# A 2-D prefix-sum diagonal kernel: the end of the last batch rearranged over blocks 30 to 32, and block 32 of the other batches loaded in one piece

## The chip, the cores and the metric

The kernel runs on one core of one Trainium2 chip. The metric is the device time of one execution in microseconds (us). A core has TensorE (PE in the profile, with its weight loads as PEld), VectorE (DVE), ScalarE (ACT), GpSimd (POOL), SyncE (SP), which here issues the loads, and 16 DMA engines. Time before: 684.33 us, median of 3 runs (683.99 to 684.5). Ratios compare runs of the same chip and rounds; where two experiments of different rounds are set side by side, the kernel before, at 684.2 to 684.4 us in all rounds, is the link.

## The reference

```python
def setup_inputs():
    B, H, W = 4, 4224, 4224
    return {"x": np.random.randn(B, H, W).astype(np.float32)}

def reference(x):
    ps = np.cumsum(np.cumsum(x, axis=1), axis=2)
    diag = np.diagonal(ps, axis1=1, axis2=2)
    return np.cumsum(diag, axis=1).astype(np.float32)
```

The output is only 4 x 4224 numbers, but all of x has to be read: 285 MB. The step from one diagonal element of the 2-D prefix sum to the next is a row sum up to the diagonal plus a column sum above the diagonal. So the kernel needs one number s per row, and then two running sums over all 4224 rows: one gives the diagonal, the next gives the output.

## The kernel before

Each batch is cut into 33 blocks of 128 rows (P = 128, W = 4224, LAST = 32). A block arrives as one tile of 128 x 4224. ScalarE sums its rows up to the diagonal block. VectorE multiplies the diagonal block with a strict upper triangle (`du`) and adds the columns to the right to a running `acc`. TensorE gets the column sums from `du` and `acc` with a vector of ones.

```python
        for I in range(NB):
            is_last = I == LAST
            xt = tiles.tile([P, W], FP32, name="xt")              # 6 buffers
            if not is_last or len(last_chunks) == 1:
                nc.sync.dma_start(out=xt, in_=x[b, P * I : P * (I + 1), :])
            else:                                                 # block 32: four pieces
                for (c0, c1) in last_chunks:                      # 256, 1792, 1920, 256 columns
                    nc.sync.dma_start(out=xt[:, c0:c1], in_=x[b, P * I : P * (I + 1), c0:c1])
            # ... ScalarE: row sums (block 32: four sums into rp_parts)
            nc.vector.tensor_tensor_reduce(out=du, in0=xt[:, P * I : P * (I + 1)], in1=u_strict,
                                           # ...
                                           accum_out=rp_du[:, I : I + 1])
            nc.tensor.matmul(cp_ps[:, I : I + 1], lhsT=du, rhs=ones_col, ...)
            if I >= 1:
                nc.tensor.matmul(cp_ps[:, I : I + 1], lhsT=acc[:, P * I : P * (I + 1)], rhs=ones_col, ...)
            # ... VectorE: acc[:, P*(I+1):] += xt[:, P*(I+1):]
```

At the end of every batch the two running sums ("pass 1" and "pass 2") are made for blocks 0 to 31 as soon as block 31 has been summed. Each pass is a chain of small matmuls with small copies between them, on ScalarE: `a_sb`, `p_sb`, then `a2_sb`, `p2_sb`. Block 32 enters at the very end, with one matmul against a ramp: the two running sums are linear in s, so row sums that come late can be added afterwards.

```python
    def cumsum_pass1(x_sb):
        nc.tensor.matmul(cs_ps, lhsT=u_incl, rhs=x_sb, start=True, stop=False)
        nc.tensor.matmul(a_ps, lhsT=x_sb, rhs=ones_col, start=True, stop=True)
        nc.scalar.copy(a_sb, a_ps)
        nc.tensor.matmul(p_ps, lhsT=a_sb, rhs=u_strict[0:NB, 0:NB], start=True, stop=True)
        nc.scalar.copy(p_sb, p_ps)
        nc.tensor.matmul(cs_ps, lhsT=ones_row, rhs=p_sb, start=False, stop=True)
        nc.vector.tensor_copy(t_sb, cs_ps)
    # ...
        nc.tensor.matmul(ot_ps[LAST : LAST + 1, :], lhsT=delta, rhs=ramp_ut, ...)   # block 32
        nc.scalar.copy(ot_sb[LAST : LAST + 1, :], ot_ps[LAST : LAST + 1, :])
        nc.scalar.dma_start(out=out_by_block[b, LAST : LAST + 1, :], in_=ot_sb[LAST : LAST + 1, :])
```

## Time and profile before

| | before |
|---|---|
| span of the profiled run | 682.8 us |
| last piece of input landed (from the DMA's semaphore in the trace) | 674.20 us |
| from there to the end | 8.6 us |
| busy: DVE, ACT, PE | 48%, 42%, 22% |

The page of the profile cuts the span into 40 slices. The DMA row gives the busy share of the 16 DMA engines in tenths, the row below what they moved in GB/s; the two lines after these are the chain of work that ended last, by engine and by what it did.

```profile
DMA  8999999999999999999999999999999999999992
GB/s 364 432 430 430 428 429 427 426 431 424 429 428 428 426 430 426 430 429 429 423 429 428 428 429 430 430 429 431 427 420 429 430 426 430 431 428 429 428 424 112
...
DMA 88%; DVE 6%; ACT 4%; issue 1%; PE 0%; SPq 0%; DVEq 0%; ACTq 0%
```

The stream of input bounds the kernel from start to end. No engine is near full. What is outside the stream is the tail. The timeline of the tail gives start, duration, engine, line, operation, result and operands with their shapes, and in brackets the idle time before it and what ended it:

```profile
669.16 3.62 ACT L138 ACTIVATE act_scratch<-xt 128x4096 bf16<-128x4096 f32 x1 [1.52 <-DMA xt<-in_x_dram]
...
672.77 0.40 ACT L146 ACTIVATE act_scratch<-xt 128x256 bf16<-128x256 f32 x1
672.90 0.19 DVE L216 TENSOR_TENSOR s_sb<-rp_full,rp_du 128x32 f32<-128x32 f32 x1 [2.98 <-ACT act_scratch L138]
...
673.17 1.68 ACT L146 ACTIVATE act_scratch<-xt 128x1792 bf16<-128x1792 f32 x1
...
675.56 1.80 ACT L146 ACTIVATE act_scratch<-xt 128x1920 bf16<-128x1920 f32 x1
...
677.75 0.13 ACT L106 COPY a_sb<-a_ps 33x1 f32<-33x1 f32 x1
...
679.14 0.26 ACT L235 COPY ot_sb<-ot_ps 32x128 f32<-32x128 f32 x1 [0.72 <-PE ot_ps L113]
...
679.45 0.59 PE L272 MATMUL ot_ps<-ramp_ut,delta 128*1 128x128 f32 x2 [0.34 <-ACT ot_sb L235]
...
680.07 0.26 ACT L280 COPY ot_sb<-ot_ps 1x128 f32<-1x128 f32 x1 [0.68 <-PE ot_ps L272]
680.36 0.21 ACTq L281 DMA_DIRECT2D out_dram<-ot_sb  x1
```

ScalarE does nearly everything in turn: block 31's sum, the four sums of block 32, and the small copies of both passes between them (`a_sb` of pass 2 has to wait until 677.75, behind the sums). The last input landed at 674.20, but the last copy ends only at 680.33, and the span 2.5 us after that.

### The profile page before, as it was taken

The numbers are of one execution on the slowest core, as the hardware profiler recorded it, in microseconds if no ns is written. First come the engines' busy times: TensorE is split into PE (matmuls) and PEld (weight loads), VectorE is DVE, ScalarE is ACT, GpSimd is POOL, SyncE is SP. The second block draws the span as 40 slices with busy tenths as digits, with TensorE's granted clock in tenths as the row PEclk, the third lists the DMA queues.
The fourth block names the chain that finished last, engine by engine and source line by source line (L and its number), as shares of the span: only waits on it lengthen the run. The fifth ranks groups of instructions, "written<-read, shape, count | busy, mean of one in ns | idle before, by whom it ended". The sixth has DMA issues, their size and how long they took to land.

```text
span 682.8 us, 2551 instructions
## 1 busy us (share of the span) xinstructions
PE 146.8 (22%) x592; PEld 129.1 (19%) x592; DVE 327.0 (48%) x432; ACT 285.8 (42%) x313; POOL 9.2 (1%) x17
## 2 busy tenths in 40 slices
PE   0121121122311211211322112112132112122123
PEld 0121121122211211211212112112121112111122
DVE  3876553321587664422167765433117766543211
ACT  1122344567312333556712223446671123345566
POOL 1000000000100000000010000000001000000000
DMA  8999999999999999999999999999999999999992
GB/s 364 432 430 430 428 429 427 426 431 424 429 428 428 426 430 426 430 429 429 423 429 428 428 429 430 430 429 431 427 420 429 430 426 430 431 428 429 428 424 112
DMA packets 20886, 285.70 MB, mean 418 GB/s; under 512 B 2372, under 2 KB 3464, under 8 KB 4488
## 3 DMA queue, kind: packets, MB, share of 16 engines
q1 hardware_dynamic: 20736, 285.48, 98.5%
q8 instruction: 4, 0.07, 0.0%
q0 software_dynamic: 128, 0.07, 0.0%
q14 instruction: 10, 0.08, 0.0%
q10 hardware_dynamic: 8, 0.00, 0.0%
HBM read 285.47 MB, written 0.07 MB: 418 GB/s over the span
## 4 chain that ended last, share of the span: by engine, by line
DMA 88%; DVE 6%; ACT 4%; issue 1%; PE 0%; SPq 0%; DVEq 0%; ACTq 0%
DMA xt<-in_x_dram 88%; DVE acc L189 5%; ACT act_scratch L138 3%; ACT act_scratch L146 1%; DVE du L154 1%; DVE acc L185 0%; SPq L129 0%; PE ot_ps L113 0%; PE ot_ps L272 0%; PE p_ps L108 0%; PE p_ps L91 0%; ACT ot_sb L235 0%; ACT ot_sb L280 0%; DVEq L154 0%; ACT p_sb L112 0%
## 5 line engine op out<-in xcount | busy, mean ns | idle before, releaser
L138 ACT ACTIVATE act_scratch<-xt 128x128 bf16<-128x128 f32 (+31 forms) x128 | 251.3, 1963 | 385.2 <-DMA xt<-in_x_dram 383.9
L189 DVE TENSOR_TENSOR acc<-acc,xt 128x3968 f32<-128x3968 f32 (+30 forms) x124 | 283.6, 2287 | 0.0
L154 DVE CUSTOM_DVE_ANT_0 du<-xt,u_strict 128x128 f32<-128x128 f32 x132 | 38.6, 292 | 322.5 <-DMA xt<-in_x_dram 322.5
L164 PE MATMUL cp_ps<-ones_col,du 128*128 128x1 f32 x264 | 77.3, 362 | 514.5 <-DVE rp_du L154 514.5
L164 PEld LDWEIGHTS cp_ps<-ones_col,du 128*128 128x128 f32 x264 | 66.3, 312 | 526.3 <-DVE rp_du L154 517.0
L174 PE MATMUL cp_ps<-ones_col,acc 128*128 128x1 f32 x256 | 72.4, 352 | 0.0
L174 PEld LDWEIGHTS cp_ps<-ones_col,acc 128*128 128x128 f32 x256 | 70.0, 333 | 0.0
L138 ACT ACTIVATION_READ_ACCUMULATOR act_scratch<-xt 128x1 f32 x128 | 23.8, 186 | 0.0
L146 ACT ACTIVATE act_scratch<-xt 128x256 bf16<-128x256 f32 (+2 forms) x16 | 17.1, 1068 | 0.0
L236 POOL DMA_DIRECT2D out_dram<-ot_sb x4 | 7.2, 1808 | 670.4 <-ACT ot_sb L235 670.4
L154 DVE DVE_READ_ACCUMULATOR2_ANT rp_du<- 128x1 f32 x132 | 10.9, 83 | 0.2
L185 DVE COPY acc<-xt 128x4096 f32<-128x4096 f32 x4 | 9.2, 2288 | 0.0
L216 DVE TENSOR_TENSOR s_sb<-rp_full,rp_du 128x32 f32<-128x32 f32 x4 | 0.8, 191 | 11.9 <-ACT act_scratch L138 11.9
L250 DVE TENSOR_TENSOR pre<-pre,rp_parts 128x1 f32<-128x1 f32 x8 | 1.3, 160 | 9.7 <-ACT act_scratch L146 9.7
L85 PE MATMUL cs_ps<-s_sb,u_incl 128*128 128x33 f32 x8 | 2.5, 412 | 8.0 <-DVE s_sb L222 8.0
L85 PEld LDWEIGHTS cs_ps<-s_sb,u_incl 128*128 128x128 f32 x8 | 2.0, 311 | 8.4 <-DVE s_sb L222 8.4
L98 DVE COPY t_sb<-cs_ps 128x33 f32<-128x33 f32 x4 | 0.8, 193 | 5.0 <-PE cs_ps L96 5.0
L146 ACT ACTIVATION_READ_ACCUMULATOR act_scratch<-xt 128x1 f32 x16 | 3.0, 186 | 0.0
L102 PE MATMUL ot_ps<-u_incl,t_sb 128*33 128x128 f32 x8 | 2.5, 421 | 1.1 <-DVE t_sb L98 1.1
L96 PE MATMUL cs_ps<-p_sb,u_incl 1*128 1x33 f32 x8 | 2.5, 408 | 1.1 <-ACT p_sb L95 1.1
L113 PE MATMUL ot_ps<-u_incl,p_sb 1*33 1x128 f32 x8 | 2.5, 417 | 1.1 <-ACT p_sb L112 1.1
L272 PE MATMUL ot_ps<-ramp_ut,delta 128*1 128x128 f32 x8 | 2.3, 397 | 1.4 <-ACT ot_sb L235 1.4
(38 smaller groups left out, 22.5 us busy)
## 6 DMA issues: line engine op xcount, KB each, us to landing
xt<-in_x_dram SPq DMA_DIRECT2D x128, 2112.0 KB, 27.2
xt<-in_x_dram SPq DMA_DIRECT2D x4, 960.0 KB, 25.8
xt<-in_x_dram SPq DMA_DIRECT2D x4, 896.0 KB, 24.1
xt<-in_x_dram SPq DMA_DIRECT2D x8, 128.0 KB, 23.9
out_dram<-ot_sb POOLq DMA_DIRECT2D x4, 16.0 KB, 7.1
out_dram<-ot_sb ACTq DMA_DIRECT2D x4, 0.5 KB
```

Source lines behind the costliest of these rows:

```text
L85: nc.tensor.matmul(cs_ps, lhsT=u_incl, rhs=x_sb, start=True, stop=False)
L96: nc.tensor.matmul(cs_ps, lhsT=ones_row, rhs=p_sb, start=False, stop=True)
L102: nc.tensor.matmul(ot_ps, lhsT=t_sb, rhs=u_incl, start=True, stop=False)
L113: nc.tensor.matmul(ot_ps, lhsT=p2_sb, rhs=ones_row, start=False, stop=True)
L138: nc.scalar.activation(out=act_scratch[:, 0 : P * (I + 1)], in_=xt[:, 0 : P * (I + 1)], func=mybir.ActivationFunctionType.Copy, accum_out= ...
L146: nc.scalar.activation(out=act_scratch[:, c0:c1], in_=xt[:, c0:c1], func=mybir.ActivationFunctionType.Copy, accum_out=rp_parts[:, ci : ci ...
L154: nc.vector.tensor_tensor_reduce(out=du, in0=xt[:, P * I : P * (I + 1)], in1=u_strict, scale=1.0, scalar=0.0, op0=mybir.AluOpType.mult, op ...
L164: nc.tensor.matmul(cp_ps[:, I : I + 1], lhsT=du, rhs=ones_col, start=False, stop=False, skip_group_check=True,)
L174: nc.tensor.matmul(cp_ps[:, I : I + 1], lhsT=acc[:, P * I : P * (I + 1)], rhs=ones_col, start=False, stop=False, skip_group_check=True,)
L185: nc.vector.tensor_copy(out=acc[:, P * (I + 1) :], in_=xt[:, P * (I + 1) :])
L189: nc.vector.tensor_tensor(out=acc[:, P * (I + 1) :], in0=acc[:, P * (I + 1) :], in1=xt[:, P * (I + 1) :], op=mybir.AluOpType.add,)
L236: nc.gpsimd.dma_start(out=out_by_block[b, 0:LAST, :], in_=ot_sb[0:LAST, :],)
```

## The change

It has two parts. In batches 0 to 2, block 32 is loaded in one piece and summed in one piece, and the passes wait for it. In the last batch the passes start from block 30 instead of block 31; blocks 31 and 32 are both added later with ramp matmuls; long row sums are shared between ScalarE and VectorE; the small copies move to VectorE; and the order on VectorE, ScalarE and TensorE is fixed by hand. The intent is a shorter way from the last landing to the last store.

```diff
-        for I in range(NB):
-            is_last = I == LAST
-            ...
-                for (c0, c1) in last_chunks:
-                    nc.sync.dma_start(out=xt[:, c0:c1], ...)
+        for I in range(NB - 3 if last_batch else NB):
+            xt = tiles.tile([P, W], FP32, name="xt")
+            nc.sync.dma_start(out=xt, in_=x[b, P * I : P * (I + 1), :])
+            row_sum(xt, 0, P * (I + 1), rp_full[:, I : I + 1])
             ...
+        # ---- the last three blocks of the last batch
+    SPLIT30, SPLIT31 = 17 * P, 24 * P
+    CH = [(22 * P, W), (0, 8 * P), (8 * P, 18 * P), (18 * P, 22 * P)]  # VectorE takes CH[1]
+            row_sum(x30, 0, SPLIT30, rp_full[:, L2 : L2 + 1])            # ScalarE
+            ...
+            sum_dve(x30, SPLIT30, P * L1, rb[:, 0:1])                    # VectorE
+            ...                                                          # s_sb of blocks 0 to 30
+            nc.tensor.matmul(cs_ps, lhsT=u_incl, rhs=s_sb, start=True, stop=False)
+            nc.tensor.matmul(a_ps, lhsT=s_sb, rhs=ones_col, start=True, stop=True)
+            nc.vector.tensor_copy(a_sb, a_ps)
+            ...                                                          # pass 1
+            row_sum(x31, 0, SPLIT31, rp_full[:, L1 : L1 + 1])
+            nc.tensor.matmul(a2_ps, lhsT=t_sb, rhs=ones_col, start=True, stop=True)
+            ot_add(ot_ps, t_sb, u_incl, start=True)
+            ot_add(ot32_ps, t_sb[:, LAST : LAST + 1], u_incl, start=True)
+            ...
+            nc.vector.tensor_copy(a2_sb, a2_ps)
+            nc.tensor.matmul(p2_ps, lhsT=a2_sb, rhs=u_strict[0:NB, 0:NB], start=True, stop=True)
+            cp_add(L1, du)
+            cp_add(L1, acc[:, P * L1 : P * LAST])
+            ...
+            ot_add(ot_ps[0:32, :], s31mat, ramp_ut, stop=True)           # block 31
+            ot_add(ot32_ps, s31, ramp_full)
+            ...
+            row_sum(x32, *CH[2], parts[2])
+            ot_add(ot32_ps, parts[2], ramp_ut)                           # block 32
+            ot_add(ot32_ps, pre, ramp_ut)
+            ...
+            row_sum(x32, *CH[3], parts[3])
+            ot_add(ot32_ps, parts[3], ramp_ut, stop=True)
+            nc.scalar.copy(ot32_sb, ot32_ps)
+            nc.scalar.dma_start(out=out_by_block[b, LAST : LAST + 1, :], in_=ot32_sb)
```

More of the change, by code (lines that the diff above doesn't have):

```diff
@@ L30 @@
     N_TILE_BUFS = 6
-    fast_tail = (LAST % 32 == 0) and NB >= 3
+    fast_tail = (LAST % 32 == 0) and NB >= 4 and B >= 1
     consts = ctx.enter_context(tc.tile_pool(name="consts", bufs=1))
@@ L63 @@
     )
-    ident = consts.tile([P, P], FP32)
-    make_identity(nc, ident)
+    ramp_full = consts.tile([P, P], FP32)
+    nc.gpsimd.iota(
+        ramp_full,
+        base=P + 1,
+        pattern=[[1, P]],
+        channel_multiplier=-1,
+        allow_small_or_imprecise_dtypes=True,
+    )
     ones_col = consts.tile([P, 1], FP32)
@@ L68 @@
     ones_row = u_incl[0:1, :]
-    if fast_tail and W > 4 * P:
-        lo = W - 2 * P
-        third = max(P, ((lo - 2 * P) // (2 * P)) * P)
-        last_chunks = [
-            (lo, W),
-            (0, third),
-            (third, lo - 2 * P),
-            (lo - 2 * P, lo),
-        ]
-        last_chunks = [(a, b) for (a, b) in last_chunks if b > a]
-    else:
-        last_chunks = [(0, W)]
+    SPLIT30, SPLIT31 = 17 * P, 24 * P
+    CH = [(22 * P, W), (0, 8 * P), (8 * P, 18 * P), (18 * P, 22 * P)]
     def cumsum_pass1(x_sb):
@@ L113, in cumsum_pass2_transposed @@
         nc.tensor.matmul(ot_ps, lhsT=p2_sb, rhs=ones_row, start=False, stop=True)
+    ADD, SUB = mybir.AluOpType.add, mybir.AluOpType.subtract
     out_by_block = out.rearrange("b (i r) -> b i r", r=P)
     for b in range(B):
+        last_batch = fast_tail and b == B - 1
         rp_full = perbatch.tile([P, NB], FP32, name="rp_full")
         rp_du = perbatch.tile([P, NB], FP32, name="rp_du")
-        rp_parts = perbatch.tile([P, 8], FP32, name="rp_parts")
         acc = perbatch.tile([P, W], FP32, name="acc")
@@ L123, with row_du @@
         nc.vector.memset(cp_ps, 0.0)
-        for I in range(NB):
-            is_last = I == LAST
-            xt = tiles.tile([P, W], FP32, name="xt")
-            if not is_last or len(last_chunks) == 1:
-                nc.sync.dma_start(out=xt, in_=x[b, P * I : P * (I + 1), :])
-            else:
-                for (c0, c1) in last_chunks:
-                    nc.sync.dma_start(
-                        out=xt[:, c0:c1], in_=x[b, P * I : P * (I + 1), c0:c1]
-                    )
-            act_scratch = scratch.tile([P, W], BF16, name="act_scratch")
-            if not is_last or len(last_chunks) == 1:
-                nc.scalar.activation(
-                    out=act_scratch[:, 0 : P * (I + 1)],
-                    in_=xt[:, 0 : P * (I + 1)],
-                    func=mybir.ActivationFunctionType.Copy,
-                    accum_out=rp_full[:, I : I + 1],
-                )
-            else:
-                for ci, (c0, c1) in enumerate(last_chunks):
-                    nc.scalar.activation(
-                        out=act_scratch[:, c0:c1],
-                        in_=xt[:, c0:c1],
-                        func=mybir.ActivationFunctionType.Copy,
-                        accum_out=rp_parts[:, ci : ci + 1],
-                    )
+        s_sb = smalls.tile([P, NB], FP32, name="s_sb")
+        ot_ps = psum_ph2.tile([NB, P], FP32, name="ot_ps")
+        ot_sb = smalls.tile([NB, P], FP32, name="ot_sb")
+        def row_du(I, xt):
             du = dupool.tile([P, P], FP32, name="du")
@@ L163, with cp_add @@
             )
+            return du
+        def cp_add(I, lhsT):
             nc.tensor.matmul(
-                cp_ps[:, I : I + 1],
-                lhsT=du,
-                rhs=ones_col,
-                start=False,
-                stop=False,
-                skip_group_check=True,
-            )
-            if I >= 1:
-                nc.tensor.matmul(
-                    cp_ps[:, I : I + 1],
-                    lhsT=acc[:, P * I : P * (I + 1)],
-                    rhs=ones_col,
-                    start=False,
-                    stop=False,
-                    skip_group_check=True,
-                )
@@ L183 @@
-            if I < NB - 1:
-                if I == 0:
-                    nc.vector.tensor_copy(
-                        out=acc[:, P * (I + 1) :], in_=xt[:, P * (I + 1) :]
-                    )
-                else:
-                    nc.vector.tensor_tensor(
-                        out=acc[:, P * (I + 1) :],
-                        in0=acc[:, P * (I + 1) :],
-                        in1=xt[:, P * (I + 1) :],
-                        op=mybir.AluOpType.add,
-                    )
-        if not fast_tail:
-            s_sb = smalls.tile([P, NB], FP32, name="s_sb")
-            nc.vector.tensor_tensor(
-                out=s_sb,
-                in0=rp_full,
-                in1=rp_du,
-                op=mybir.AluOpType.subtract,
-            )
-            nc.vector.tensor_tensor(
-                out=s_sb, in0=s_sb, in1=cp_ps, op=mybir.AluOpType.add
-            )
+                cp_ps[:, I : I + 1], lhsT=lhsT, rhs=ones_col,
@@ new lines, in cp_add, with acc_add, row_sum @@
+                start=False, stop=False, skip_group_check=True,
+            )
+        def acc_add(I, xt):
+            if I == 0:
+                nc.vector.tensor_copy(out=acc[:, P:], in_=xt[:, P:])
+            else:
+                nc.vector.tensor_tensor(
+                    out=acc[:, P * (I + 1) :],
+                    in0=acc[:, P * (I + 1) :],
+                    in1=xt[:, P * (I + 1) :],
+                    op=ADD,
+                )
+        def row_sum(xt, c0, c1, out):
+            act_scratch = scratch.tile([P, W], BF16, name="act_scratch")
+            nc.scalar.activation(
+                out=act_scratch[:, c0:c1],
+                in_=xt[:, c0:c1],
+                func=mybir.ActivationFunctionType.Copy,
+                accum_out=out,
+            )
@@ new lines @@
+        for I in range(NB - 3 if last_batch else NB):
+            xt = tiles.tile([P, W], FP32, name="xt")
+            nc.sync.dma_start(out=xt, in_=x[b, P * I : P * (I + 1), :])
+            row_sum(xt, 0, P * (I + 1), rp_full[:, I : I + 1])
+            du = row_du(I, xt)
+            cp_add(I, du)
+            if I >= 1:
+                cp_add(I, acc[:, P * I : P * (I + 1)])
+            if I < NB - 1:
+                acc_add(I, xt)
+        if not last_batch:
+            nc.vector.tensor_tensor(out=s_sb, in0=rp_full, in1=rp_du, op=SUB)
+            nc.vector.tensor_tensor(out=s_sb, in0=s_sb, in1=cp_ps, op=ADD)
@@ L207 @@
             t_sb = cumsum_pass1(s_sb)
-            ot_ps = psum_ph2.tile([NB, P], FP32, name="ot_ps")
             cumsum_pass2_transposed(t_sb, ot_ps)
-            ot_sb = smalls.tile([NB, P], FP32, name="ot_sb")
             nc.scalar.copy(ot_sb, ot_ps)
@@ L213 @@
             continue
-        s_sb = smalls.tile([P, NB], FP32, name="s_sb")
-        nc.vector.tensor_tensor(
-            out=s_sb[:, 0:LAST],
-            in0=rp_full[:, 0:LAST],
-            in1=rp_du[:, 0:LAST],
-            op=mybir.AluOpType.subtract,
-        )
-        nc.vector.tensor_tensor(
-            out=s_sb[:, 0:LAST],
-            in0=s_sb[:, 0:LAST],
-            in1=cp_ps[:, 0:LAST],
-            op=mybir.AluOpType.add,
-        )
-        nc.vector.memset(s_sb[:, LAST : LAST + 1], 0.0)
@@ L230 @@
-        t_sb = cumsum_pass1(s_sb)
-        ot_ps = psum_ph2.tile([NB, P], FP32, name="ot_ps")
-        cumsum_pass2_transposed(t_sb, ot_ps)
-        ot_sb = smalls.tile([NB, P], FP32, name="ot_sb")
-        nc.scalar.copy(ot_sb[0:LAST, :], ot_ps[0:LAST, :])
-        nc.gpsimd.dma_start(
-            out=out_by_block[b, 0:LAST, :],
-            in_=ot_sb[0:LAST, :],
-        )
-        npart = len(last_chunks)
-        pre = smalls.tile([P, 1], FP32, name="pre")
-        nc.vector.tensor_tensor(
-            out=pre,
-            in0=rp_parts[:, 0:1],
-            in1=rp_du[:, LAST : LAST + 1],
-            op=mybir.AluOpType.subtract,
-        )
@@ L249 @@
-        for ci in range(1, npart - 1):
-            nc.vector.tensor_tensor(
-                out=pre,
-                in0=pre,
-                in1=rp_parts[:, ci : ci + 1],
-                op=mybir.AluOpType.add,
-            )
-        nc.vector.tensor_tensor(
-            out=pre,
-            in0=pre,
-            in1=cp_ps[:, LAST : LAST + 1],
-            op=mybir.AluOpType.add,
-        )
-        delta = smalls.tile([P, 1], FP32, name="delta")
-        if npart > 1:
-            nc.vector.tensor_tensor(
-                out=delta,
-                in0=pre,
-                in1=rp_parts[:, npart - 1 : npart],
-                op=mybir.AluOpType.add,
-            )
-        else:
-            delta = pre
@@ L272 @@
-        nc.tensor.matmul(
-            ot_ps[LAST : LAST + 1, :],
-            lhsT=delta,
-            rhs=ramp_ut,
-            start=False,
-            stop=True,
-            skip_group_check=True,
-        )
-        nc.scalar.copy(ot_sb[LAST : LAST + 1, :], ot_ps[LAST : LAST + 1, :])
-        nc.scalar.dma_start(
-            out=out_by_block[b, LAST : LAST + 1, :],
-            in_=ot_sb[LAST : LAST + 1, :],
-        )
+        ET = mybir.EngineType
+        L1, L2 = LAST - 1, LAST - 2
@@ new lines @@
+        s31mat = smalls.tile([P, 32], FP32, name="s31mat")
+        s31 = smalls.tile([P, 1], FP32, name="s31")
+        pre = smalls.tile([P, 1], FP32, name="pre")
+        rb = smalls.tile([P, 8], FP32, name="rb")
+        parts = [smalls.tile([P, 1], FP32, name=f"part{k}") for k in range(4)]
+        ot32_ps = psum_ph2.tile([1, P], FP32, name="ot32_ps")
+        cp32_ps = psum_ph2.tile([P, 1], FP32, name="cp32_ps")
+        ot32_sb = smalls.tile([1, P], FP32, name="ot32_sb")
+        x30 = tiles.tile([P, W], FP32, name="xt")
@@ new lines, with sum_dve, ot_add @@
+        nc.sync.dma_start(out=x30, in_=x[b, P * L2 : P * L1, :])
+        x31 = tiles.tile([P, W], FP32, name="xt")
+        nc.sync.dma_start(out=x31, in_=x[b, P * L1 : P * LAST, :])
+        x32 = tiles.tile([P, W], FP32, name="xt")
+        for (c0, c1) in CH:
+            nc.sync.dma_start(out=x32[:, c0:c1], in_=x[b, P * LAST :, c0:c1])
+        def sum_dve(xt, c0, c1, out):
+            nc.vector.reduce_sum(out, xt[:, c0:c1], axis=mybir.AxisListType.X)
+        def ot_add(out, lhsT, rhs, start=False, stop=False):
+            nc.tensor.matmul(out, lhsT=lhsT, rhs=rhs, start=start, stop=stop,
+                             skip_group_check=True)
@@ new lines @@
+        with tc.manual_schedule(engines={ET.DVE, ET.Activation, ET.PE}):
+            nc.vector.memset(s31mat, 0.0)
+            nc.vector.memset(s_sb[:, L1 : LAST + 1], 0.0)
+            row_sum(x30, 0, SPLIT30, rp_full[:, L2 : L2 + 1])
+            du = row_du(L2, x30)
+            acc_add(L2, x30)
+            cp_add(L2, du)
+            cp_add(L2, acc[:, P * L2 : P * L1])
+            sum_dve(x30, SPLIT30, P * L1, rb[:, 0:1])
+            nc.vector.tensor_tensor(out=s_sb[:, 0:L1], in0=rp_full[:, 0:L1], in1=rp_du[:, 0:L1], op=SUB)
+            nc.vector.tensor_tensor(out=s_sb[:, 0:L1], in0=s_sb[:, 0:L1], in1=cp_ps[:, 0:L1], op=ADD)
+            nc.vector.tensor_tensor(out=s_sb[:, L2:L1], in0=s_sb[:, L2:L1], in1=rb[:, 0:1], op=ADD)
+            cs_ps = psum_ph2.tile([P, NB], FP32, name="cs_ps")
+            nc.tensor.matmul(cs_ps, lhsT=u_incl, rhs=s_sb, start=True, stop=False)
+            a_ps = psum_ph2.tile([NB, 1], FP32, name="a_ps", tag="aux_ps")
+            nc.tensor.matmul(a_ps, lhsT=s_sb, rhs=ones_col, start=True, stop=True)
+            a_sb = smalls.tile([NB, 1], FP32, name="a_sb")
+            nc.vector.tensor_copy(a_sb, a_ps)
+            p_ps = psum_ph2.tile([1, NB], FP32, name="p_ps", tag="aux_ps")
+            nc.tensor.matmul(p_ps, lhsT=a_sb, rhs=u_strict[0:NB, 0:NB], start=True, stop=True)
+            p_sb = smalls.tile([1, NB], FP32, name="p_sb")
+            nc.vector.tensor_copy(p_sb, p_ps)
+            nc.tensor.matmul(cs_ps, lhsT=ones_row, rhs=p_sb, start=False, stop=True)
+            t_sb = smalls.tile([P, NB], FP32, name="t_sb")
+            nc.vector.tensor_copy(t_sb, cs_ps)
+            row_sum(x31, 0, SPLIT31, rp_full[:, L1 : L1 + 1])
+            a2_ps = psum_ph2.tile([NB, 1], FP32, name="a2_ps", tag="aux_ps")
+            nc.tensor.matmul(a2_ps, lhsT=t_sb, rhs=ones_col, start=True, stop=True)
+            ot_add(ot_ps, t_sb, u_incl, start=True)
+            ot_add(ot32_ps, t_sb[:, LAST : LAST + 1], u_incl, start=True)
+            du = row_du(L1, x31)
+            acc_add(L1, x31)
+            a2_sb = smalls.tile([NB, 1], FP32, name="a2_sb")
+            nc.vector.tensor_copy(a2_sb, a2_ps)
+            p2_ps = psum_ph2.tile([1, NB], FP32, name="p2_ps", tag="aux_ps")
+            nc.tensor.matmul(p2_ps, lhsT=a2_sb, rhs=u_strict[0:NB, 0:NB], start=True, stop=True)
+            cp_add(L1, du)
+            cp_add(L1, acc[:, P * L1 : P * LAST])
+            p2_sb = smalls.tile([1, NB], FP32, name="p2_sb")
+            nc.vector.tensor_copy(p2_sb, p2_ps)
+            ot_add(ot_ps, p2_sb, ones_row)
+            ot_add(ot32_ps, p2_sb[:, LAST : LAST + 1], ones_row)
+            du = row_du(LAST, x32)
+            nc.tensor.matmul(cp32_ps, lhsT=du, rhs=ones_col, start=True, stop=False)
+            nc.tensor.matmul(cp32_ps, lhsT=acc[:, P * LAST :], rhs=ones_col, start=False, stop=True)
+            sum_dve(x31, SPLIT31, P * LAST, rb[:, 1:2])
+            nc.vector.tensor_tensor(out=s31, in0=rp_full[:, L1:LAST], in1=rp_du[:, L1:LAST], op=SUB)
+            nc.vector.tensor_tensor(out=s31, in0=s31, in1=cp_ps[:, L1:LAST], op=ADD)
+            nc.vector.tensor_tensor(out=s31, in0=s31, in1=rb[:, 1:2], op=ADD)
+            nc.vector.tensor_copy(out=s31mat[:, 31:32], in_=s31)
+            row_sum(x32, *CH[0], parts[0])
+            ot_add(ot_ps[0:32, :], s31mat, ramp_ut, stop=True)
+            ot_add(ot32_ps, s31, ramp_full)
+            sum_dve(x32, *CH[1], parts[1])
+            nc.vector.tensor_tensor(out=pre, in0=parts[0], in1=rp_du[:, LAST : LAST + 1], op=SUB)
+            nc.vector.tensor_tensor(out=pre, in0=pre, in1=cp32_ps, op=ADD)
+            nc.vector.tensor_tensor(out=pre, in0=pre, in1=parts[1], op=ADD)
+            row_sum(x32, *CH[2], parts[2])
+            ot_add(ot32_ps, parts[2], ramp_ut)
+            ot_add(ot32_ps, pre, ramp_ut)
+            nc.vector.tensor_copy(ot_sb[0:LAST, :], ot_ps[0:LAST, :])
+            nc.gpsimd.dma_start(out=out_by_block[b, 0:LAST, :], in_=ot_sb[0:LAST, :])
+            row_sum(x32, *CH[3], parts[3])
+            ot_add(ot32_ps, parts[3], ramp_ut, stop=True)
+            nc.scalar.copy(ot32_sb, ot32_ps)
+            nc.scalar.dma_start(out=out_by_block[b, LAST : LAST + 1, :], in_=ot32_sb)
```

## The prediction

> **What bounds the kernel now.** The DMA stream. The page's slices show the 16 DMA engines at 9 tenths or more almost throughout and 424–432 GB/s in nearly every slice. The Trainium skill, "DMA: Bandwidth & Descriptors", Specifications, gives 435 GB/s as the fabric ceiling; the trace agrees (about 429). The chain of waits is 88% DMA of xt. DVE (48%), ACT (42%) and PE (22%) have slack. The last input lands at 674.2 us (DMA packets) and the span ends at 682.8 us, so only 8.6 us, 1.3%, lie outside the stream.
>
> **The tail before (timeline).** ACT gets block 31 at 669.16 and needs 3.6 us, then the four parts of block 32 to 677.85 (with both passes' copies); pass 2 ends with ot_sb at 679.40, the ramp matmul (0.60) and the copy at 680.33. From there 2.5 us to the end (row's store landing, closing).
>
> **What the change does.**
> 1. Batches 0–2 load block 32 in one piece, not four. A row costs 634 ns as one packet and 46+279+295+46 = 666 ns as four; 8 rows per engine make 0.25 us per batch, with semaphore packets about 0.28: 0.8 us earlier end of the stream. On the path.
> 2. Those batches lose the early pass: block 32's ACT sum (3.7 us) now comes before s_sb, so DVE reaches the next batch some 2–3 us later. Six buffers (27 us issue to landing) cover this: no cost.
> 3. Last batch: passes 1 and 2 start from block 30 instead of 31, their small copies move to DVE, long row sums are split ACT/DVE, and blocks 31/32 enter by linearity through ramp matmuls. Added: about 8 small matmuls (0.43 us apart), DVE ops of 0.16 us (0.25 apart when dependent), three reduces.
>
> **Costing the new tail** on the old clock (block 30 lands 663.95, block 31 at 669.07). The Trainium skill, "VectorE: DVE Perf Modes", the perf-mode tier table, has tensor_reduce at 1x; no reduce is in this trace, so I estimate it at the pace of the f32 acc add (1.04 ns per column: 1792 columns 2.0, 1024 columns 1.15 us). DVE: block 30's reduce ends 666.6, s_sb 667.4, t_sb 669.9, p2_sb 671.6, block 31's reduce 673.0, s31mat 673.9, part 1's reduce 675.1, pre 675.8. ACT: block 31's 3072 columns end 672.0, then 1408, 1280 and 512 columns: 673.5, 675.0, 675.7. PE: pre at 675.8, part 3 at 676.25–676.85, copy to 677.15, end 679.6. So the tail shortens by 3.2 us, bound by DVE and PE rather than ACT, still not by the last landing. With the 0.8 us of point 1: span about 678.8.
>
> **Prediction:** 680.4 us (684.33 minus about 4.0, -0.6%), range 679.0 to 681.8. Faster by over 2%: 0.01; within 2%: 0.98; slower: 0.01. 2% (13.7 us) exceeds the whole tail.
>
> **What would show it.** DMA packets: last landing about 673.4. Timeline of the tail: final ACT copy ending near 676.4; last PE matmuls waiting for DVE's pre as much as for ACT's part 3. Batch edges: GB/s no lower than before. Chain of waits: last 10 us through DVE/PE instead of ACT's sums. DVE busy up 4 us, ACT down 3.
>
> **What would make it wrong.** A reduce slower than 1.04 ns per column (each 0.5 ns/column adds about 1 us after block 31); the extra PE queue behind the row-32 matmuls; DVE's delay at batch edges starving the DMA queue; the 16 KB store from POOL landing late (7.1 us mid-stream, 1.6 us in the old tail).

## The result, and the profile after

The changed kernel takes 679.76 us (median of 10 runs, 679.56 to 680.03), the kernel before 684.32 us (12 runs of the same rounds). The ratio is 0.9934, with a 95% interval of 0.9924 to 0.9943: 0.7% faster, which counts as "the same" at a threshold of 2%. A ratio here is the mean time of one kernel's runs over that of the other's of the same rounds, so it is not quite the ratio of the quoted medians.

The lines of the page after that answer to those of before:

```profile
DMA  8999999999999999999999999999999999999995
GB/s 366 431 430 430 428 428 424 430 430 429 429 428 428 431 429 424 431 428 430 427 429 431 429 425 429 429 429 429 429 430 425 431 429 428 427 429 430 428 429 209
...
DMA 86%; DVE 7%; ACT 5%; PE 2%; issue 1%; SPq 0%; DVEq 0%; ACTq 0%
```

The stream looks the same; only its last slice is fuller, because the end comes sooner. The end of the chain of waits of the changed kernel (start in us, duration, what it was), from block 30's landing on:

```profile
663.80 2.01 DVE rb L206
...
666.45 0.64 PE cs_ps L227 x2
...
669.00 0.27 PE a_ps L242 x2
669.27 0.99 PE ot_ps L209 x4
670.26 0.20 PE p_ps L250 x2
670.46 0.94 PE cp_ps L141 x4
671.40 1.07 PE ot_ps L209 x4
672.47 0.52 PE cp_ps L258 x2
672.99 0.43 PE cp_ps L259 x2
673.41 2.28 PE ot_ps L209 x10
```

ScalarE's sums are gone from the chain. It goes through VectorE's share of block 30, pass 1, and then through TensorE without a gap from 669.00 to 675.69: small matmuls, one behind the other. The last steps of the timeline show that it is a close race there:

```profile
674.05 0.61 ACT L159 ACTIVATE act_scratch<-xt 128x512 bf16<-128x512 f32 x1
674.20 0.13 PEld L209 LDWEIGHTS ot_ps<-ramp_ut,part 128*1 128x1 f32 x2 [0.30 <-ACT act_scratch L159]
674.20 0.63 PE L209 MATMUL ot_ps<-ramp_ut,part 128*1 128x128 f32 x2
674.21 0.16 DVE L272 TENSOR_TENSOR pre<-pre,part 128x1 f32<-128x1 f32 x1
...
674.62 0.63 PE L209 MATMUL ot_ps<-ramp_ut,pre 128*1 128x128 f32 x2
...
675.05 0.64 PE L209 MATMUL ot_ps<-ramp_ut,part 128*1 128x128 f32 x2
675.72 0.25 ACT L280 COPY ot_sb<-ot_ps 1x128 f32<-1x128 f32 x1 [0.96 <-PE ot_ps L209]
676.00 0.49 ACTq L281 DMA_DIRECT2D out_dram<-ot_sb  x1
```

The three matmuls of block 32 start 0.43 us apart. ScalarE's sum of the second-last chunk ended at 674.14, VectorE's `pre` at 674.37, ScalarE's last sum at 674.75; TensorE was free for them at 674.20, 674.62 and 675.05.

The gain of 4.8 us of span divides by three times that stand in both traces (block 30's landing of the last batch from the DMA's semaphore, the end of the last copy, the end of the span):

| stretch | before | after | difference | predicted |
|---|---|---|---|---|
| start to landing of block 30 | 663.95 | 663.11 | -0.84 | -0.8 |
| landing of block 30 to end of the last copy | 16.38 | 12.86 | -3.52 | -3.2 |
| end of the last copy to the end of the span | 2.47 | 2.01 | -0.46 | 0 |

### One late DMA engine

One thing in both profiles had not been part of the prediction. The views by windows near the end (stretch, length, busy time of PE, PEld, DVE, ACT, POOL with counts, clock, DMA share, GB/s) show how the stream ends, before and after:

```profile
670.00:671.00 1.00, 1.00 (x6) 1.00 (x6) 0.00 (x0) 1.00 (x1) 0.00 (x0) 1.00 0.39 156
...
672.00:673.00 1.00, 0.00 (x0) 0.00 (x0) 0.10 (x1) 1.00 (x3) 0.00 (x0) 1.00 0.06 23
673.00:674.00 1.00, 0.57 (x3) 0.50 (x3) 0.35 (x3) 1.00 (x3) 0.00 (x0) 1.00 0.04 16
```

```profile
669.00:670.00 1.00, 1.00 (x6) 0.38 (x6) 0.46 (x4) 1.00 (x1) 0.00 (x0) 1.00 0.46 185
...
671.00:672.00 1.00, 1.00 (x5) 0.58 (x6) 1.00 (x2) 1.00 (x2) 0.00 (x0) 1.00 0.06 26
672.00:673.00 1.00, 1.00 (x5) 0.60 (x4) 0.83 (x6) 0.67 (x3) 0.00 (x0) 1.00 0.06 22
```

A DMA share of 0.06 is one engine of 16. In the changed kernel 15 engines have delivered everything at 671.45, and the last one lands at 673.34. The trace has 16 semaphore updates for each load, so it shows for every block how late each of the 16 is. Sorted lateness against the first one (us), worked out from those counts for the changed kernel, with the instruction fetches that the trace shows in between (q8 and q14 are the queues marked "instruction" on the page; the figure in ns is how long their packet took):

```
block landed at 8.8    0.0 0.0 0.1 0.2 0.2 0.2 0.2 0.2 0.2 0.3 0.3 0.3 0.3 0.4 0.6 0.9
  fetch at  83.4 q14, 325 ns
block landed at 84.9   ...                                     0.4 0.4 0.5 0.6 0.9 1.3
  fetches at 114.1 (q14, 309 ns), 124.4 (q8, 1099 ns), 194.5 (q14, 309 ns), 245.9 (q14, 325 ns)
block landed at 247.4  ...                                     0.5 0.8 1.0 1.1 1.8 2.4
  fetches at 267.0 (q8), 321.7 (q14, 309 ns)
block landed at 398.9  ...                                     0.6 1.2 1.5 1.9 2.4 2.5
  fetch at 402.7 (q14, 326 ns)
block landed at 404.8  ...                                     0.6 1.2 1.6 1.9 2.5 3.4
  fetches at 414.2 (q8), 518.8, 519.9 (q14, 309 ns), 555.1 (q8), 565.2 (q14, 325 ns)
block landed at 567.2  0.0 0.1 0.2 0.2 0.2 0.4 0.4 0.6 0.6 1.6 1.8 1.8 1.9 2.2 2.5 4.3
```

The lists are sorted and name no engine, so they are best read one against the next. Between the blocks landed at 398.9 and 404.8 the entry 2.39 goes and 3.36 comes, while 2.53 stays: read as one entry moved, one engine lost 0.97 us at that fetch, and it had not been the last one until then. Each of the four packets of 325 or 326 ns moves one entry back in this way, by 0.97 to 1.04 us (0.2 to 1.2, 1.3 to 2.3, 2.4 to 3.4, 3.4 to 4.3), and no later list shows it catching up. The packets of 1.0 to 1.1 us (q8) move an entry back by about 1.5 us and those of 309 ns one by about 0.7 us, but each time one from another place in the list, so that none of these ends last. Why a packet of 0.33 us costs its engine three times as much stays open. The kernel before shows the same: fetches of 325 to 333 ns at 83.6, 236.3, 383.2 and 535.8, and 4.4 us at the end. In the changed kernel they come about every 160 us, and about 130 of VectorE's 565 program entries pass in that time (an estimate, 565 x 160 / 678). That made VectorE's instructions the suspect, to be tested.

### The profile page after: what moved, and what is told of

Read it like the earlier page. It is cut to its first block, busy times and chain, and to the rows that moved or that the text cites. A ratio compares the mean times of both kernels' runs of the same rounds, so it can differ in the third digit from the quotient of the medians.

```text
span 678.0 us, 2501 instructions
## 1 busy us (share of the span) xinstructions
PE 148.2 (22%) x598; PEld 130.0 (19%) x598; DVE 330.3 (49%) x426; ACT 279.7 (41%) x285; POOL 4.0 (1%) x16
## 4 chain that ended last, share of the span: by engine, by line
DMA 86%; DVE 7%; ACT 5%; PE 2%; issue 1%; SPq 0%; DVEq 0%; ACTq 0%
DMA xt<-in_x_dram 86%; DVE acc L150 5%; ACT act_scratch L159 5%; PE ot_ps L209 1%; DVE du L128 1%; DVE acc L148 0%; DVE rb L206 0%; SPq L168 0%; PE cp_ps L141 0%; PE cs_ps L93 0%; PE cs_ps L236 0%; PE cs_ps L82 0%; PE cs_ps L227 0%; PE cp_ps L258 0%; PE cp_ps L259 0%
## 5 line engine op out<-in xcount | busy, mean ns | idle before, releaser
L159 ACT ACTIVATE act_scratch<-xt 128x1280 bf16<-128x1280 f32 (+11 forms) x134 | 263.4, 1965 | 381.7 <-DMA xt<-in_x_dram 381.7
L159 ACT ACTIVATION_READ_ACCUMULATOR act_scratch<-xt 128x1 f32 x134 | 25.0, 186 | 0.0
L183 POOL DMA_DIRECT2D out_dram<-ot_sb x3 | 1.7, 575 | 511.8 <-ACT ot_sb L182 511.8
L206 DVE TENSOR_REDUCE rb<-xt 128x1 f32<-128x1792 f32 (+1 forms) x2 | 3.2, 1606 | 0.0
L93 PEld LDWEIGHTS cs_ps<-p_sb,u_incl 1*128 1x128 f32 x6 | 1.5, 308 | 1.4 <-ACT p_sb L92 1.4
```

The source lines that it names most:

```text
L159: nc.scalar.activation(out=act_scratch[:, c0:c1], in_=xt[:, c0:c1], func=mybir.ActivationFunctionType.Copy, accum_out=out,)
L183: nc.gpsimd.dma_start(out=out_by_block[b], in_=ot_sb)
L206: nc.vector.reduce_sum(out, xt[:, c0:c1], axis=mybir.AxisListType.X)
```

## The experiments

Ten kernels ran, and all gave correct results. "Before" in each line is the kernel before in the same rounds.

### e1_loads_only: the loads alone

```diff
-            if not is_last or len(last_chunks) == 1:
+            if not is_last or b < B - 1:
                 nc.sync.dma_start(out=xt, in_=x[b, P * I : P * (I + 1), :])
```

> The kernel before, with block 32 of batches 0 to 2 loaded in one piece; sums and tail unchanged. Theory (the removed packets are on the path): block 30 of the last batch lands 0.8 us earlier and the whole run is 0.8 us shorter, 683.5 us. Rival (the whole gain comes from the rewritten tail, the stream's end is set by something else than these packets): 684.3 us, no change.

Measured: 683.49 us (683.46 to 683.66) against 684.35 before, 0.86 us less; the ratio is 0.9988, and its interval (0.9976 to 1.0001) just includes 1, so the timing alone leaves a little doubt. The trace adds that block 30 of the last batch lands at 663.00 instead of 663.95. The theory holds, the rival does not explain the earlier landing. This kernel still makes the early pass at the edges of batches 0 to 2, and the changed kernel, which does not, has its block 30 at 663.11: giving up the early pass cost at most 0.1 us.

### e2_tail_only: the new tail alone

```diff
-            nc.sync.dma_start(out=xt, in_=x[b, P * I : P * (I + 1), :])
+            if I < NB - 1:
+                nc.sync.dma_start(out=xt, in_=x[b, P * I : P * (I + 1), :])
+            else:
+                for (c0, c1) in [(31 * P, W), (0, 14 * P), (14 * P, 29 * P), (29 * P, 31 * P)]:
+                    nc.sync.dma_start(out=xt[:, c0:c1], in_=x[b, P * I : P * (I + 1), c0:c1])
```

> The changed kernel, with block 32 of batches 0 to 2 loaded in the four pieces of before. Theory: 0.8 us over the changed kernel, 680.6 us, with the tail after block 30's landing as in the changed kernel (14.8 us to the end). Rival (the gain is all tail): 679.8 us. Together with the run of the loads alone the two parts should add up to the measured 4.6 us; a gap would mean that they interact.

Measured: 680.91 us (680.6 to 680.98) against 684.35 before, ratio 0.9949: 3.44 us less. It is 1.15 us above the changed kernel's median (from other rounds); the spans in the two traces differ by 1.19 us. Of that, 0.82 us is block 30's landing (663.93 against 663.11). Another 0.37 us is the stretch from the landing of the last store to the end of the span, 1.25 against 0.89 us. The two parts add up to 0.86 + 3.44 = 4.30 us, against 4.56 us for both at once. That last stretch is where the gap comes from: in the traces it is 0.05 us shorter than before in e1, 0.12 us in this run and 0.49 us with both (more on it below, under point 5 of why the prediction was right).

### e3_dve_dose: more VectorE instructions

```diff
             if I < NB - 1:
                 acc_add(I, xt)
+            for _ in range(3):
+                nc.vector.tensor_copy(dummy, du[:, 0:1])
```

> The changed kernel with three more tiny VectorE copies per block (about 390 instructions more, output unchanged, VectorE off the critical path in the stream). Theory: one DMA engine also fetches VectorE's instructions, falls back by 0.7 to 1.0 us at each fetch (4 fetches so far, at 83, 246, 403 and 565 us, and it ends alone, 1.8 us after the other 15); with some 70% more VectorE instructions there are about 7 fetches, the last landing comes about 2.5 us later, and the run is 2 to 3 us longer, about 682.3 us. Rival (that engine is just slow, or the lag has another cause): number of instructions without effect on landings, 679.8 us.

Measured: 682.78 us (682.57 to 682.84) against 684.35 before, ratio 0.9977: 3.0 us above the changed kernel. There are now seven packets of 325 to 333 ns in the instruction queue (at 53, 145, 236, 333, 425, 516 and 608 us), the late engine is 7.0 us behind the first at the end (each packet again moves one entry back by about 1.0 us), and 15 engines are done at 671.36, as before, while the last lands at 676.22. The view by windows shows it: one engine alone from 671 on.

```profile
671.00:672.00 1.00, 0.71 (x4) 0.58 (x5) 0.36 (x4) 0.82 (x1) 0.00 (x0) 1.00 0.05 23
...
674.00:675.00 1.00, 1.00 (x6) 0.47 (x5) 0.97 (x2) 1.00 (x2) 0.00 (x0) 1.00 0.06 26
```

Tiny copies on an engine with idle time, worth nothing by the busy shares, cost 3 us at the far end. The rival falls.

### e4_probe: which engine it is

```diff
+        for k in (15, 14, 12, 8, 4, 10):
+            nc.sync.dma_start(out=probe[0:k, k - 1, :], in_=x[b, 0:k, 0:P])
```

> The changed kernel with six small loads of 15, 14, 12, 8, 4 and 10 rows queued behind the last chunks, to see which DMA engine is the late one. If a small load of n rows runs on the n lowest engines, then all loads whose engines include the late one complete after about 672.9 us, the others up to 1.8 us earlier. Highest engine late: all six early. If rows were spread some other way, no such border shows. Run time about that of the changed kernel, or up to 1 us more.

Measured: 680.04 us in a single look. The Trainium skill, "DMA: Bandwidth & Descriptors", "Why a DMA increments its semaphore by 16 and not by 1", says that a load issued here goes to the lowest-numbered engines, as many as divide its rows. The trace agrees in the counts: the load of 8 rows has eight separate arrivals, the load of 4 rows four (671.34, 671.36, 672.36 and 674.45 us). All six loads complete late, at 673.7 to 674.6 us, the one of four rows too. So the late engine is among the lowest four, if the page is right about which engines are used, and a last load on four or more engines cannot avoid it. I did not find out which of the four it is.

### e5_fewer_dve: fewer VectorE instructions

`tensor_tensor_reduce` is two instructions, one that computes and one that reads the accumulator. Here the product is a plain multiply, and one reduce does the row sums of up to 17 blocks:

```diff
-            du = row_du(I, xt)
-            cp_add(I, du)
+            nc.vector.tensor_tensor(out=du8[:, g, :], in0=xt[:, P * I : P * (I + 1)], in1=u_strict, op=mult)
+            cp_add(I, du8[:, g, :])
             ...
+            if I in lasts:      # 16, 28, 32; in the last batch 16, 25, 29
+                nc.vector.reduce_sum(rp_du[:, I - g : I + 1], du8[:, 0 : g + 1, :], axis=X)
```

> The changed kernel, with the masked product of each block as one plain VectorE multiply into a buffer of 17 blocks and their row sums taken by three reduces per batch: 334 VectorE instructions in the program in place of 565; the last three blocks as in the changed kernel. Theory (fetches of VectorE's instructions hold up one DMA engine, 0.7 to 1.0 us each): 2, at most 3, fetches before the end of the stream instead of 4, last landing 1 to 1.8 us earlier (the next engines are 2.5 us behind the first, the late one 4.3), run 678.0 to 678.8 us. Rival (the dose run lengthened the stream by something else than fetches, such as busier VectorE): VectorE is about as busy here, so 679.8 us, no change.

Measured: 678.02 us (677.86 to 678.22) against 684.36 before, ratio 0.9907: 1.7 us below the changed kernel. VectorE is busier (346.9 us against 330.3), but has 309 instead of 426 instructions in the profile. Its fetches come at 108.4, 392.6 and 671.5 us, so only two inside the stream, and the last landing is at 671.79 instead of 673.34, with 15 engines done at 671.27 again. A block counts as landed when the last of the 16 is done, so in the changed kernel the late engine had held back every block since the fetch at 402.7 us: block 30 of the last batch, with which the tail starts, now lands at 661.51 instead of 663.11, which is nearly the whole gain.

```profile
670.00:671.00 1.00, 1.00 (x7) 0.69 (x6) 0.50 (x4) 1.00 (x3) 0.00 (x0) 1.00 0.24 93
```

```profile
670.00:671.00 1.00, 1.00 (x6) 0.40 (x4) 0.65 (x4) 0.89 (x2) 0.00 (x0) 1.00 0.21 81
...
672.00:673.00 1.00, 1.00 (x7) 0.29 (x5) 0.86 (x5) 1.00 (x4) 0.00 (x0) 1.00 0.00 0
```

Up to 671 the two are alike; at 672 nothing is left to land in the second. Busier and faster: the rival (busy time on VectorE) falls with the other sign, too.

### e6_fewer_dve_pe and e9_fewer_dve_pe2: fewer TensorE instructions as well

```diff
-            cp_add(I, du8[:, g, :])
-            if I >= 1:
-                cp_add(I, acc[:, P * I : P * (I + 1)])
             ...
+                nc.vector.tensor_tensor(out=du8[:, o : g + 1, :], in0=du8[:, o : g + 1, :],
+                    in1=acc[:, P * lo : P * (I + 1)].rearrange("p (k c) -> p k c", c=P), op=ADD)
+                for J in range(I - g, I + 1):
+                    cp_add(J, du8[:, J - (I - g), :])
```

> The same, and the accumulated slices are added to the masked products on VectorE, 17 blocks at a time, so that TensorE does one small matmul per block in place of two (TensorE program 185 instead of 310 entries, two 16 KB fetches expected in place of four). Theory: the engines 1.6 to 2.5 us behind come forward too; the last landing is then set by whichever has most fetches left; 0 to 0.7 us below the run before, 677.5 to 678.5 us. Rival: only VectorE's fetches matter: equal to the run before.

Measured: 678.94 us (678.77 to 679.17) against 684.36 before, ratio 0.9921. That is 0.9 us slower than e5, and the expectation was wrong. TensorE's busy time fell from 148.2 to 77.0 us, and its 16 KB fetches from four to two, as the lines of the DMA queues show for both (queue, kind: packets, MB, share):

```profile
q8 instruction: 4, 0.07, 0.0%
```

```profile
q8 instruction: 2, 0.03, 0.0%
```

But the merge had put 9 entries on VectorE's program (343 against 334), and its third fetch moved from 671.5 to 667.9 us. The late engine went from 2.5 to 3.4 us behind the first between the landings of the first and the second chunk of block 32, and the last landing was 672.50. (The next expectation says "from 2.1"; that was the second-last engine, misread.) And the next three engines did not come forward: when block 31 landed they were 2.0, 2.0 and 2.1 us behind the first, against 1.8, 2.0 and 2.2 in e5. But besides the late one only four engines, and not six as in e5, were more than 1.4 us behind at the end: two fewer, with two fewer 16 KB fetches.

To test that reading, the groups of batches 0 to 2 were made 17 and 16 blocks (from 17, 12 and 4), which brings the program to 334 again:

```diff
-        firsts = (0, 17, 26) if last_batch else (0, 17, 29)
+        firsts = (0, 17, 26) if last_batch else (0, 17)
```

> The run with one small matmul per block again (it came out 0.9 us slower than the run without that merge, against the expectation, and its trace shows a third VectorE fetch at 667.9 us, just inside the stream, and the late engine falling from 2.1 to 3.4 us there). Here the groups of batches 0 to 2 are 17 and 16 blocks, which takes 9 instructions out of VectorE's program (334, as in the kernel that had its third fetch after the stream). Theory: the third fetch moves behind the last landing, the last landing comes about 1 us earlier than in that run, 677.9 to 678.1 us. Rival (the merge itself costs, through VectorE or through bursts of matmuls): 678.9 us or more.

Measured: 678.17 us (677.91 to 678.76) against 684.21 before, ratio 0.9911; third fetch at 671.4 us, last landing at 671.74. The place of one fetch explains the loss. The saved matmuls themselves gained nothing that can be seen against e5 (678.02).

### e7_no_split: no sharing of row sums

```diff
-    SPLIT30, SPLIT31 = 17 * P, 24 * P
+    SPLIT30, SPLIT31 = 31 * P, 32 * P
-            sum_dve(x30, SPLIT30, P * L1, rb[:, 0:1])        # and the same for block 31,
-            ...                                              # and the adds of rb
```

> The changed kernel, with ScalarE summing all columns of the blocks 30 and 31 alone (both shared VectorE reduces gone). Theory (the tail is a chain that starts at block 30's row sum and runs through the passes without slack): s_sb comes 0.9 us later and everything after it, 680.7 us. Rival (only what follows the last chunk counts, ScalarE's sums of block 32): ScalarE has 0.85 us more to sum in block 31 and ends 0.6 us later, 680.2 us to 680.4 us, and the TensorE queue has gaps.

Measured: 680.73 us (680.66 to 680.99) against 684.36 before, ratio 0.9947: 1.0 us above the changed kernel, as the theory has it, and not the 0.4 to 0.6 us of the rival. In its chain of waits ScalarE's sum of block 30 stands in place of VectorE's, and then TensorE again, with no gap:

```profile
663.29 3.61 ACT act_scratch L159 x2
...
667.46 0.64 PE cs_ps L225 x2
...
674.42 2.28 PE ot_ps L209 x10
```

The final group starts at 674.42 instead of 673.41: the 1.0 us is handed down from block 30 to the end without loss.

### e8_copies_on_act: the small copies on ScalarE

```diff
-            nc.vector.tensor_copy(a_sb, a_ps)     # and p_sb, a2_sb, p2_sb
+            nc.scalar.copy(a_sb, a_ps)
```

> The changed kernel, with the four small copies of passes 1 and 2 (a, p, a2, p2) on ScalarE again, as before the change. Theory: those of pass 1 cost nothing (ScalarE is idle then), those of pass 2 wait behind ScalarE's sum of block 31, so a2 comes 1.7 us later, TensorE uses part of that time for the other matmuls, and the end is 0.5 us later, 680.3 us. Rival (slack there): 679.8 us.

Measured: 680.8 us (680.62 to 681.02) against 684.36 before, ratio 0.9948: 1.0 us above the changed kernel, so the direction is the theory's and the size is twice its 0.5 us. The timeline shows why:

```profile
671.33 0.14 ACT L248 COPY a_sb<-a_ps 33x1 f32<-33x1 f32 x1
...
671.52 0.27 PE L250 MATMUL p_ps<-u_strict,a_sb 33*1 33x33 f32 x2 [1.01 <-ACT a_sb L248]
...
671.71 0.59 PE L141 MATMUL cp_ps<-ones_col,du 128*128 128x1 f32 x2
```

`a2` waits behind ScalarE's sum of block 31, as expected. But TensorE does not use the time. The order is fixed by hand, and it takes its instructions in order: block 31's two column sums, whose operands had been ready for more than a microsecond, stand behind the matmul that waits for `a2`. TensorE is idle for 1.01 us, and this is the loss. (The profiled run, at 681.02 us, is the slowest of the five; its span is 1.33 us longer than the changed kernel's, of which block 30's landing, at 663.37 instead of 663.11, is 0.26.)

### e10_fewer_dve_split: e5 with another split of block 30

```diff
-    SPLIT30, SPLIT31 = 17 * P, 24 * P
+    SPLIT30, SPLIT31 = 19 * P, 24 * P
```

> The kernel with fewer VectorE instructions, and ScalarE takes 19 instead of 17 column blocks of block 30's row sum. Theory (the tail is a chain through block 30's VectorE reduce and TensorE's queue, with 0.25 us until ScalarE's last sum would bound it): the sums of both engines meet 0.27 us earlier and the end follows by 0.25 us: 677.8 us. Rival (ScalarE's last sums of block 32 already bound it): 678.0 us.

Measured: 677.91 us (677.86 to 677.99) against 684.21 before, ratio 0.9907. This is 0.1 us below e5, from other rounds, and can't be told from it. The trace says more. From block 30's landing to the first step of `s_sb` it took 2.44 us against 2.51 in e5 (2.62 in the changed kernel), because ScalarE's longer sum now ended after VectorE's. From the landing to the end of the last matmul it took 12.54 against 12.53 in e5 (12.58 in the changed kernel). So the start gained 0.07 us of the expected 0.27 and the end nothing. That fits the rival: the last three matmuls begin with the one that waits for ScalarE's sum of the second-last chunk, and ScalarE was waiting for that chunk to land (0.29 us idle in e5, 0.30 here). With so small a gain at the start, though, the run is a weak test of it.

```profile
671.09 1.27 ACT L160 ACTIVATE act_scratch<-xt 128x1280 bf16<-128x1280 f32 x1 [0.30 <-DMA xt<-in_x_dram]
...
672.51 0.09 PEld L220 LDWEIGHTS ot_ps<-ramp_ut,part 128*1 128x1 f32 x2 [0.49 <-ACT act_scratch L160]
```

This kernel has the lowest median of all kernels here, 0.9% below the kernel before.

## Why the prediction was right

The time was predicted as 680.4 us (679.0 to 681.8) and measured as 679.76 us. Point by point:

1. The stream bounds the kernel, and the change has only the tail and some packets to work on. Right: the chain of waits is 86% DMA after, and the whole gain is 4.6 us of a stretch of 8.6 us plus the packets.
2. One-piece loads, 0.8 us: right. Block 30 lands 0.84 us earlier, and e1 measures 0.86 us for this part alone.
3. No cost at the edges of batches 0 to 2: right. e1 and the changed kernel have their block 30 within 0.11 us of each other. The loads did wait for ScalarE more (79.9 against 30.9 us in the waits of the load queue), without effect.
4. The new tail, 3.2 us: the mechanism was right, and the measured 3.5 us is near it. The path ran through VectorE's reduce of block 30, pass 1 and TensorE's queue, as costed. The reduces took 2.01 us (1792 columns) and 1.20 us (1024 columns) against the estimates of 2.0 and 1.15 us; so the 1x for tensor_reduce of the Trainium skill, "VectorE: DVE Perf Modes", the perf-mode tier table, agrees: the two differ by 0.81 us over 768 columns, 1.05 ns per column. The prediction let TensorE's last matmuls wait for `pre`, at 675.0 when the estimate is moved by 0.8 us; `pre` was ready at 674.37, TensorE's own queue set the end, and it came 0.3 us sooner. "Bound by DVE and PE rather than ACT" was half right: TensorE's queue is what the chain shows, and the weight load at 674.20 shows that ScalarE's sum of the second-last chunk arrives at almost the same moment. Sharing the sums and moving the copies were each taken back by a run (e7 and e8, 1.0 us each); the earlier start of the passes was not taken back alone, so its share of the 3.4 us is not shown.
5. "From there 2.5 us to the end" was taken as fixed. It was 2.01 us after. This term was mis-sized by 0.46 us, and it is the largest part of the remaining difference. From the last store's landing to the end of the span it took 1.38 us before, 1.33 in e1, 1.25 in e2, 1.02 in e4 and 0.89 to 0.90 in the changed kernel and the other runs. The packed trace also has the waiting instructions, which the views leave out, and they account for it. At the end SyncE checks the semaphores of the DMAs in a fixed order, one step every 0.06 us. The steps that are left when the last store lands number 5 before, 6 in e1 and e2, 3 in e4 and 1 in the others: up to 0.36 us more after the landing. The rest is one late step of another engine: VectorE's closing step at 682.46 us adds 0.23 us before, ScalarE's at 681.43 us 0.12 us in e1. So about half of the 0.46 us is which semaphore the last store happened to use, a side effect that nobody planned; why VectorE's step was late stays open. This is read from the traces, and no run was made to test it.
6. Busy times: VectorE up by 3.3 us (4 predicted), ScalarE down by 6.1 us (3 predicted). The prediction had left out that batches 0 to 2 also lose sums: the four sums of block 32 took 5.0 us per batch ((17.1 + 3.0) / 4 on the page), one sum of 4224 columns about 3.9 us, an estimate from the 3.62 us and 0.19 us of 4096 columns. None of this is on the path.
7. Late store from POOL, DMA starved at the edges, slower reduce: none of the named dangers occurred. The 16 KB store landed at 676.5 us, before the other.

What the prediction did not see is that the end of the stream is not set by all 16 DMA engines but by one, which is 1.9 us behind the other 15 at the end and holds back the landing of every block since about 400 us. The change leaves this as it was (4.4 us behind the first before, 4.3 us after), so it did no harm to the number. e3, e5, e6 and e9 show its cause: the fetches of VectorE's instructions.

## What to carry to other kernels

When a kernel is bound by a DMA stream that never pauses, look at how the stream ends: if the last landings come from one engine alone, something small has been delaying that engine all along, and here it was the fetching of instructions by an engine that was half idle. Fewer instructions there gained 1.7 us, half of the 3.4 us that the whole rewritten tail gained. And in a tail, cost the chain from the landing that starts it, engine by engine with the durations of the old trace, and keep work that is ready ahead of work that waits in an in-order queue: the sum came within 0.4 us, and the one misordered wait of e8 cost 1 us.

## What the Trainium skill lacked or had wrong

- "Runtime: NRT & Kernel Launch", "Instruction fetch mechanics", says that instructions are refilled in 16 KiB blocks by the sequencer's own DMA queue, and that the cost is mostly hidden. The 16 KB packets are there (four of 1.0 to 1.1 us; two when TensorE's program was cut from 310 to 185 entries). VectorE's fetches inside the stream were packets of 8 KB and 325 to 336 ns. Hidden they may be for the engine that fetches, but not for a stream that keeps all DMA engines busy: each of VectorE's put one DMA engine about 1.0 us further behind for good. Seven of them instead of four cost 3.0 us; two instead of four gained 1.7 us.
- "DMA: Bandwidth & Descriptors", "Latency and other measured facts", names engines 7 and 15 as usually the slower ones (and ties that to loads issued from GpSimd, which the input stream here is not). Here the late one is among the lowest four, by e4_probe and the page's own rule for small loads, and it starts level with the others (the first fetch moves an entry that was about 0.2 us behind; at the end it is 4.3 us).
- No page that I found says that the end of a saturated stream can be set by one engine: 15 engines were done at 671.2 to 671.5 us in the changed kernel, e3, e5, e9 and e10, and the last landing was at 673.34, 676.22, 671.79, 671.74 and 671.88 us.
